# Nine of a trunk's projections read their 512 moving columns, and write their bank, in another order

## The chip, the cores and the metric

One core of a Trainium2 chip runs the whole program. The time is device microseconds of one execution; the median of three runs of the kernel before is 717.47 us (717.14 to 718.04). One further execution was recorded by the hardware profiler. Engines are named as in its profile: PE is TensorE's matmuls, PEld its loads of the stationary operand, DVE is VectorE, ACT is ScalarE, POOL is GpSimd, SP is SyncE.

## The reference

A trunk of two layers on a sequence of 512 tokens of width 1024: a Mamba-2 mixer, then a differential attention layer on shared keys and values, and a last norm. Cut to what the change touches, the mixer's input projection and what becomes of its parts:

```python
h = rms_norm(x, norm_g)
zxbcdt = h @ w_in                         # (512, 1024) @ (1024, 6176)
z   = zxbcdt[..., :2048]                  # the gate
xbc = zxbcdt[..., 2048:2048 + 4096]       # x, B and C of 8 groups
dt_raw = zxbcdt[..., 2048 + 4096:]
xbc = silu(causal_depthwise_conv(xbc, conv_w, conv_b))
...
y = ssd_chunked_scan(xs * dt[..., None], a * dt, bm, cm)
y = gated_group_rms_norm(y + d_skip * xs, z, gate_norm_g)
x = x + y @ w_out
```

All in float32. The attention layer that follows computes `softmax(A1) - lambda * softmax(A2)` on its scores, and is not touched.

## The kernel before

Every large product is made of three matmuls of rounded operands. Weights and activations are split into a high part (`whi`, `a_hi`), which is the value rounded to the type `float32r`, and the rest (`wlo`, `a_lo`). `mm3` (line 242) adds high by high, high by low and low by high into one bank of PSUM. A matmul has a stationary operand of 128 x 128 (`lhsT`), which a weight load brings in, and a moving one of 128 partitions and up to 512 columns (`rhs`); its 128 x 512 result fills one bank.

The gate projection is done in four parts, z0 to z3, each of 512 features (`z_proj`, line 475). For each of four blocks of 128 tokens a bank `pz` is filled: stationary are 128 tokens of the activations, moving are the 512 columns of a weight tile, over eight slices of the depth, so 4 x 8 x 3 = 96 matmuls in a part. ACT reads such a bank in two halves of 256 columns (`z_out`).

The group projection is done for eight groups, g0 to g7 (`group_proj`, line 498). For each of four blocks of 128 features (B, C and two halves of x) a bank `pg` is filled, the other way round: stationary are 128 columns of a weight tile, moving are the 512 tokens of the activations, again 96 matmuls in a group. `conv` then has DVE multiply the bank by a row of scales in place, and ACT and DVE make the causal convolution from it, which needs the tokens in order.

Both write into banks of the tag `mm`, of which there are four. The order of the dense work is the list `order_a`: z0 g0 g1 z1 g2 g3 z2 g4 o0 g5 z3 g6 g7 o1 o2 o3, where o0 to o3 are parts of the out projection (`po`). Around it the scan of each group (`ssd`) puts its small matmuls in between, by a scheduler which works from priorities and estimated times. z0 is partly written out by hand ahead of this list. The weights come by DMA from SP's queue, two or three pieces ahead; ACT makes their high part and DVE the rest.

The names of the profile's rows are the tiles': `pg<-a_hi,whi` is a matmul into a bank of a group projection from the high activations (moving) and the high weights (stationary), while in `pz<-whi,a_hi` the weights move. The operands are given moving first. All TensorE instructions have the one line 55, that of a helper which passes them on, so the rows are told apart by tiles.

Of the kernel before, what the change touches and what calls it, by code (L numbers as in the profile page):

```python
# [37 lines left out]

C_GA, C_GK, C_GB, C_GG, C_SG, C_DTB, C_AL, C_CB, C_CW = 0, 8, 16, 24, 40, 41, 42, 43, 75
N_PAR = 203  # L40

N_DEC = R * NQ * P + 2 * R

# [20 lines left out]
def trunk(ctx, tc, x, x_t, par, w_dt, w_in, w_out, w_kvqg, w_bo, d_skip, lam_qk, fin_g, out):  # L64
# [10 lines left out]
    def mm_bank(name):  # L75
        return psum.tile([P, 512], F32, tag="mm", name=name, bufs=4)
# [22 lines left out]
    nc.scalar.dma_start(prm[:], par[:, 0:C_CB])  # L99
    prc = const.tile([P, N_PAR - C_CB], F32, name="prc")  # L100
    x_tok = res.tile([P, NT, D], F32, name="x_tok")
# [23 lines left out]
    def load(i):  # L125
# [33 lines left out]
        if i == 0:  # L159
# [12 lines left out]
            for i in range(2, 4):  # L172
                nc.sync.dma_start(xt[i], x_t[:, 2 * i:2 * i + 2, :])
                nc.sync.dma_start(nxt[:, 2 * i - 4:2 * i - 2, :].rearrange("p k n -> p (k n)"), src1[:, (2 * i - 4) * w:(2 * i - 2) * w])
            nc.sync.dma_start(prc[:], par[:, C_CB:N_PAR])
        elif i not in begun:
# [15 lines left out]
    def use(seg):  # L192
        fetch(segs.index(seg) + 3)
        return ready.pop(seg)
# [44 lines left out]
                at = 0  # L239
            yield n  # L240

    def mm3(ps, lhs, rhs, first, last, **kw):
        (lh, ll), (rh, rl) = lhs, rhs
        T.matmul(ps, lhsT=lh, rhs=rh, start=first, stop=False, **kw)
        T.matmul(ps, lhsT=lh, rhs=rl, start=False, stop=False, **kw)
        T.matmul(ps, lhsT=ll, rhs=rh, start=False, stop=last, **kw)
# [94 lines left out]
    def new_h(tag):  # L341
        return [res.tile([P, KD, S], F32R, tag=f"hT_{i}", name=f"{tag}_{i}") for i in ("hi", "lo")]


    def tok_mm(ps, t, b, w):
        tk = slice(t * P, (t + 1) * P)
        for k in range(4):
            kk = 4 * b + k
            mm3(ps, (hh[:, kk, tk], hl[:, kk, tk]), (w[0][:, k, :], w[1][:, k, :]), b == 0 and k == 0, b == 1 and k == 3)
            yield  # L350

    hh, hl = new_h("a")
# [10 lines left out]
    def z_out(j, t, ps):  # L363

        for i in range(2):
            zs = bp2.tile([P, 256], F32, tag="zs", name=f"zs{j}_{t}_{i}", bufs=12)
            A.activation(zs, ps[:, i * 256:(i + 1) * 256], AF.Silu, scale=r_col[:, t:t + 1])
            zt[2 * j + i, t] = zs
# [15 lines left out]
    first = load(0)()  # L384
# [8 lines left out]
    for k in range(4):  # L393
        for t in range(NT):
            tk = slice(t * P, (t + 1) * P)
            mm3(pz0[t], (hh[:, k, tk], hl[:, k, tk]), (wh[:, k, :], wl[:, k, :]), k == 0, False)
# [64 lines left out]
    for t in range(NT):  # L461
        run(tok_mm(pz0[t], t, 1, w0))
        z_out(0, t, pz0[t])
# [11 lines left out]
    def z_proj(j):  # L475
        pz = [mm_bank(f"pz{j}_{t}") for t in range(NT)]
        for b in range(2):
            w = use(("z", j, b))
            for t in range(NT):
                yield from tok_mm(pz[t], t, b, w)  # L480
                if b:
                    z_out(j, t, pz[t])

    def conv(ps, ft, name, bufs):
        xc = bp2.tile([P, S], F32, tag=f"xc_{name}", name=f"xc{ft}", bufs=bufs)
        at = C_CW - C_CB + 4 * ft
        cw = [prc[:, at + k:at + k + 1] for k in range(4)]

        u = ps
        V.tensor_tensor(out=u, in0=ps, in1=r_row, op=ALU.mult)  # L490
        A.activation(xc, u, AF.Identity, scale=cw[3], bias=prc[:, ft:ft + 1])
        for k in (2, 1, 0):
            d = 3 - k
            V.scalar_tensor_tensor(out=xc[:, d:], in0=u[:, :S - d], scalar=cw[k], in1=xc[:, d:], op0=ALU.mult, op1=ALU.add)
        A.activation(xc, xc, AF.Silu)
        return xc

    def group_proj(g):
        pg = [mm_bank(f"pg{g}_{i}") for i in range(4)]
        fts = [(16 + g, "b", 1), (24 + g, "c", 2), (2 * g, "x0", 1), (2 * g + 1, "x1", 1)]  # L500
        outs = []
        for b in range(2):
            wh, wl = use(("g", g, b))
            for i in range(4):
                cs = slice(i * P, (i + 1) * P)
                for k in range(4):
                    kk = 4 * b + k
                    mm3(pg[i], (wh[:, k, cs], wl[:, k, cs]), (hh[:, kk, :], hl[:, kk, :]),
                        b == 0 and k == 0, b == 1 and k == 3)
                    yield  # L510
                if b:
                    outs.append(conv(pg[i], *fts[i]))
        conv_out[g] = outs
# [20 lines left out]
    def stream_a():  # L534
        for it in order_a[1:]:
            j = int(it[1])
            yield from {"z": z_proj, "g": group_proj, "o": out_proj}[it[0]](j)
            done.add(it)
        while True:
            yield  # L540
# [136 lines left out]
    hh, hl = new_h("b")  # L677
# [323 lines left out]
    last = None  # L1001
    for h in range(DH):
        for t in range(NT):
# [14 lines left out]
            last = h, t  # L1018
# [135 lines left out]
```

## Time and profile before

| what | value |
|---|---|
| time, median of 3 runs | 717.47 us (717.14 to 718.04) |
| time of the profiled execution | 716.54 us |
| its span, first to last instruction | 714.8 us |
| instructions in the span | 10905 |
| DMA, mean over the span | 99 GB/s |

How to read the rows that are shown below. A line of the page's first part has an engine's busy time, its share of the span and the number of instructions. The lines of the chain follow the work that ended last back to the start, and give each engine's and each tile's share of the span. A row of the waits has who waited for whom, the sum in us, how often, and the longest. A row of a group has line, engine, operation, tiles, shapes and count, then the busy time in us, the mean duration of one in ns, and the idle time before. A row of the timeline has start and duration in us, then the instruction. Matmuls overlap in a pipeline, and the profile models their ends, so two successive starts say more of TensorE's pace than a duration does. A row of the windows has a stretch of the span and each engine's busy time in it.

### The profile page before, as it was taken

The numbers are of one execution on the slowest core, as the hardware profiler recorded it, in microseconds if no ns is written. First come the engines' busy times: TensorE is split into PE (matmuls) and PEld (weight loads), VectorE is DVE, ScalarE is ACT, GpSimd is POOL, SyncE is SP. The second block draws the span as 40 slices with busy tenths as digits, with TensorE's granted clock in tenths as the row PEclk, the third lists the DMA queues.
The fourth block names the chain that finished last, engine by engine and source line by source line (L and its number), as shares of the span: only waits on it lengthen the run. The fifth ranks groups of instructions, "written<-read, shape, count | busy, mean of one in ns | idle before, by whom it ended". The sixth has DMA issues, their size and how long they took to land.

```text
span 714.8 us, 10905 instructions
## 1 busy us (share of the span) xinstructions
PE 705.8 (99%) x4030; PEld 590.2 (83%) x4030; DVE 520.0 (73%) x1195; ACT 429.9 (60%) x953; POOL 113.6 (16%) x158
## 2 busy tenths in 40 slices
PE   8999999999999999999999999999999999999996
PEld 7788888888888888888888879888988898889884
DVE  5579954889579569567996857567667857785886
ACT  6849662754734536537536357667767766756556
POOL 0108512403306025041110101000000000000002
PEclk9999999999999999999999999999999999999999
DMA  8643323233223331331222310412311131122003
GB/s 297 250 175 121 119 73 132 90 119 118 63 114 118 119 117 61 118 119 59 64 85 89 118 59 18 161 66 67 110 61 60 63 116 59 60 89 89 30 0 118
DMA packets 13061, 70.88 MB, mean 99 GB/s; under 512 B 1744, under 2 KB 2512, under 8 KB 5584
## 3 DMA queue, kind: packets, MB, share of 16 engines
q1 hardware_dynamic: 12720, 69.90, 27.3%
q8 instruction: 32, 0.52, 0.3%
q10 hardware_dynamic: 288, 0.28, 0.1%
q14 instruction: 21, 0.17, 0.1%
HBM read 68.02 MB, written 2.16 MB: 98 GB/s over the span
## 4 chain that ended last, share of the span: by engine, by line
PE 96%; DVE 1%; DMA 1%; ACT 0%; issue 0%; SPq 0%
PE pg L55 25%; PE po L55 16%; PE pz L55 12%; PE pt L55 8%; PE pv L55 6%; PE pq L55 6%; PE pk L55 6%; PE pb L55 3%; PE sc L55 3%; PE pyd L55 2%; PE pc L55 2%; PE pcb L55 1%; PE pxt L55 1%; PE psA L55 1%; PE pyt L55 1%; DMA xt<-in_x_t 1%
## 5 line engine op out<-in xcount | busy, mean ns | idle before, releaser
L55 DVE SCALAR_TENSOR_TENSOR wlo<-raw,prm,whi 128x512 fp32r<-128x512 f32 (+1 forms) x256 | 150.5, 636 | 56.3 <-ACT whi L55 56.0
L55 ACT ACTIVATE whi<-raw,prm 128x512 fp32r<-128x512 f32 (+1 forms) x256 | 136.8, 606 | 64.7 <-issue 13.8
L55 PE MATMUL pg<-a_hi,whi 128*128 128x512 f32 x256 | 103.4, 404 | 0.0
L55 PE MATMUL pg<-a_lo,whi 128*128 128x512 f32 x256 | 102.5, 400 | 0.0
L55 PE MATMUL pg<-a_hi,wlo 128*128 128x512 f32 x256 | 101.3, 401 | 0.0
L55 DVE SCALAR_TENSOR_TENSOR xc<-pg,prc,xc 128x511 f32<-128x511 f32 (+2 forms) x96 | 69.9, 740 | 7.5 <-ACT xc L55 7.1
L55 PEld LDWEIGHTS pg<-a_hi,wlo 128*128 128x128 f32 x256 | 48.1, 188 | 11.1
L55 PEld LDWEIGHTS pg<-a_hi,whi 128*128 128x128 f32 x256 | 48.2, 188 | 11.1 <-ACT zs L55 0.2
L55 PEld LDWEIGHTS pg<-a_lo,whi 128*128 128x128 f32 x256 | 48.2, 188 | 10.9
L55 PE MATMUL po<-whi,yh 128*128 128x512 f32 x128 | 51.2, 400 | 0.4 <-ACT yh L55 0.4
L55 PE MATMUL po<-wlo,yh 128*128 128x512 f32 x128 | 51.3, 401 | 0.0
L55 PE MATMUL po<-whi,yl 128*128 128x512 f32 x128 | 50.6, 399 | 0.0
L55 PE MATMUL pz<-wlo,a_hi 128*128 128x512 f32 x128 | 50.1, 400 | 0.0
L55 PE MATMUL pz<-whi,a_hi 128*128 128x512 f32 x128 | 49.4, 400 | 0.5 <-ACT a_hi L55 0.5
L55 PE MATMUL pz<-whi,a_lo 128*128 128x512 f32 x128 | 49.4, 395 | 0.0
L965 POOL TENSOR_TENSOR ot<-x_tok,fg 128x512 f32<-128x512 f32 x4 | 5.0, 1298 | 248.0 <-DVE x_tok L55 248.0
L55 ACT ACTIVATE s<-s,mx 128x128 f32<-128x128 f32 (+3 forms) x64 | 35.5, 556 | 9.6 <-DVE mx L55 9.1
L592 POOL TENSOR_TENSOR xe<-xdt,tok 128x256 f32<-128x256 f32 x24 | 14.1, 613 | 164.1 <-DVE xdt L55 164.1
L55 ACT ACTIVATE xc<-pg,prc 128x512 f32<-128x512 f32 x32 | 24.8, 776 | 24.7 <-DVE pg L55 19.5
L55 DVE CUSTOM_DVE_ANT_0 s<-sc,bias 128x128 f32<-128x128 f32 (+3 forms) x64 | 29.3, 487 | 11.9 <-PE sc L55 11.5
L55 PE MATMUL pv<-whi,b_hi 128*128 128x256 f32 x128 | 36.6, 286 | 0.0
L55 PE MATMUL pv<-wlo,b_hi 128*128 128x256 f32 x128 | 35.7, 279 | 0.0
(238 smaller groups left out, 1678.9 us busy)
## 6 DMA issues: line engine op xcount, KB each, us to landing
raw<-in_w_in SPq DMA_DIRECT2D x22, 1024.0 KB, 4.8
raw<-in_w_kvqg SPq DMA_DIRECT2D x16, 1024.0 KB, 4.7
dec<-acs_d SPq DMA_DIRECT2D x8, 1024.0 KB, 4.8
raw<-in_w_out SPq DMA_DIRECT2D x8, 1024.0 KB, 4.7
raw<-in_w_bo SPq DMA_DIRECT2D x4, 1024.0 KB, 4.8
x_tok<-in_x SPq DMA_DIRECT2D x4, 512.0 KB, 8.8
out<-ot SPq DMA_DIRECT2D x7, 256.0 KB, 2.4
raw<-in_w_in SPq DMA_DIRECT2D x4, 256.0 KB, 4.9
```

Source lines behind the costliest of these rows:

```text
L55: i = op(*args, **kw)
L592: GP.tensor_tensor(out=xe[:, c], in0=xdt[:, c], in1=toe_tok[:, c, hs].unsqueeze(2).to_broadcast([P, R, HD]), op=ALU.mult)
L965: GP.tensor_tensor(out=o, in0=y, in1=f, op=ALU.mult)
```

## The change

`mm3` gets an optional form, a pair (b, c). With it, the moving operand (high and low) and the bank are viewed in another order: the 512 columns are cut into a x b runs of c neighbouring columns, a = 512 / (b c), and the walk goes over b outside, over a in the middle, and over the c columns of a run inside. Moving columns and bank columns are permuted alike, so each result lands where it did. With (2, 4), for instance, a matmul takes columns 0 to 3, 8 to 11, 16 to 19 and so on to the end, and then 4 to 7, 12 to 15 and so on. With (16, 16) it takes 0 to 15, 256 to 271, 16 to 31, 272 to 287 and so on.

Three gate projections (z1, z2, z3) and six group projections (g1 to g6) get a form; z0, g0, g7 and all else stay as they are.

| projection | z1 | z2 | z3 | g1 | g2 | g3 | g4 | g5 | g6 |
|---|---|---|---|---|---|---|---|---|---|
| form (b, c) | 2, 4 | 2, 16 | 16, 16 | 2, 8 | 2, 4 | 2, 32 | 32, 8 | 2, 16 | 2, 128 |
| runs in a matmul, 512 / c | 128 | 32 | 32 | 64 | 128 | 16 | 64 | 32 | 4 |

```diff
+FORM_Z = {1: (2, 4), 2: (2, 16), 3: (16, 16)}
+FORM_G = {1: (2, 8), 2: (2, 4), 3: (2, 32), 4: (32, 8), 5: (2, 16), 6: (2, 128)}
...
-    def mm3(ps, lhs, rhs, first, last, **kw):
+    def walk(ap, form):
+
+        b, c = form
+        return ap.rearrange("p (a b c) -> p b a c", b=b, c=c)
+
+    def mm3(ps, lhs, rhs, first, last, form=None, **kw):
         (lh, ll), (rh, rl) = lhs, rhs
+        if form:
+            ps, rh, rl = walk(ps, form), walk(rh, form), walk(rl, form)
         T.matmul(ps, lhsT=lh, rhs=rh, start=first, stop=False, **kw)
...
-    def tok_mm(ps, t, b, w):
+    def tok_mm(ps, t, b, w, form=None):
...
-            mm3(ps, (hh[:, kk, tk], hl[:, kk, tk]), (w[0][:, k, :], w[1][:, k, :]), b == 0 and k == 0, b == 1 and k == 3)
+            mm3(ps, (hh[:, kk, tk], hl[:, kk, tk]), (w[0][:, k, :], w[1][:, k, :]), b == 0 and k == 0, b == 1 and k == 3, form)
...
-                yield from tok_mm(pz[t], t, b, w)
+                yield from tok_mm(pz[t], t, b, w, FORM_Z.get(j))
...
-                        b == 0 and k == 0, b == 1 and k == 3)
+                        b == 0 and k == 0, b == 1 and k == 3, FORM_G.get(g))
```

On TensorE the program before has, where g1 ends and z1 begins (with two matmuls of a scan, `po`, in between), these rows; a row's last part is the shape of what is moved.

```order
L55 MATMUL pg_3_633<-a_hi,wlo_545 128x512
L55 MATMUL pz_0_918<-whi_636,a_hi 128x512
L55 MATMUL po_735<-hst_684,xc_585 128x256 x2
L55 MATMUL pz_0_918<-wlo_637,a_hi 128x512
L55 MATMUL pz_0_918<-whi_636,a_lo 128x512
```

The changed program has at the same place:

```order
L58 MATMUL pg_3_633<-a_hi,wlo_545 128x2x32x8
L58 MATMUL pz_0_918<-whi_636,a_hi 128x2x64x4
L58 MATMUL po_735<-hst_684,xc_585 128x256 x2
L58 MATMUL pz_0_918<-wlo_637,a_hi 128x2x64x4
L58 MATMUL pz_0_918<-whi_636,a_lo 128x2x64x4
```

No row moved. Line numbers shift, and 512 columns have become three loops, 2 x 32 x 8 in g1 and 2 x 64 x 4 in z1. It is the same along all of TensorE: 864 matmuls have another shape, and their order, like that of every other engine's instructions and of the DMAs, is the order of before.

## The prediction

> **What bounds the kernel now.** I read the page's first part, then its chain, then the waits of TensorE, to see whether a nanosecond on a matmul is a nanosecond on the end.
>
> ```profile
> PE 705.8 (99%) x4030; PEld 590.2 (83%) x4030; DVE 520.0 (73%) x1195; ACT 429.9 (60%) x953; POOL 113.6 (16%) x158
> ```
>
> ```profile
> PE 96%; DVE 1%; DMA 1%; ACT 0%; issue 0%; SPq 0%
> PE pg L55 25%; PE po L55 16%; PE pz L55 12%; PE pt L55 8%; PE pv L55 6%; PE pq L55 6%; PE pk L55 6%; PE pb L55 3%; PE sc L55 3%; PE pyd L55 2%; PE pc L55 2%; PE pcb L55 1%; PE pxt L55 1%; PE psA L55 1%; PE pyt L55 1%; DMA xt<-in_x_t 1%
> ```
>
> ```profile
> PE warm L55 <- POOL ident masks.py:199: 1.5, 1, 1.5
> PE pz L55 <- ACT a_hi L55: 0.5, 1, 0.5
> PE po L55 <- ACT yh L55: 0.4, 1, 0.4
> ```
>
> The chain that ended last is TensorE for 96% of the span, and all that TensorE ever waits for is 1.5 + 0.5 + 0.4 = 2.4 us, none of it inside a projection that the change touches (the 0.5 stands before the first gate projection, z0). The chain's share of "issue" is 0%, so fetching or decoding matmuls is not what sets their pace. The two families that change, `pg` (group projections) and `pz` (gate projections), hold 25% and 12% of the chain. So what counts is the time from one matmul's start to the next one's (the pitch) in these families.
>
> The clock cannot be the lever, because it is granted almost in full:
>
> ```profile
> core 0: 714.8 us, clock 0.998
> ```
>
> The durations on the page (about 400 ns for 512 columns) overlap each other, so I take the pitch from the timeline, first and last row of an undisturbed stretch:
>
> ```profile
> 39.76 0.40 PE L55 MATMUL pg<-a_hi,whi 128*128 128x512 f32 x1
> ...
> 43.96 0.40 PE L55 MATMUL pg<-a_hi,whi 128*128 128x512 f32 x1
> ```
>
> There are 18 steps between these rows: 4.20 / 18 = **233.3 ns** for 512 columns, 0.456 ns a column.
>
> **How many matmuls change.**
>
> ```profile
> L55 PE MATMUL pg<-a_hi,whi 128*128 128x512 f32 x256 | 103.4, 404 | 0.0
> L55 PE MATMUL pg<-a_lo,whi 128*128 128x512 f32 x256 | 102.5, 400 | 0.0
> L55 PE MATMUL pg<-a_hi,wlo 128*128 128x512 f32 x256 | 101.3, 401 | 0.0
> ...
> L55 PE MATMUL pz<-wlo,a_hi 128*128 128x512 f32 x128 | 50.1, 400 | 0.0
> L55 PE MATMUL pz<-whi,a_hi 128*128 128x512 f32 x128 | 49.4, 400 | 0.5 <-ACT a_hi L55 0.5
> L55 PE MATMUL pz<-whi,a_lo 128*128 128x512 f32 x128 | 49.4, 395 | 0.0
> ```
>
> `pg` has 3 x 256 = 768 matmuls in 8 projections, `pz` 3 x 128 = 384 in 4: 96 in each. Six of the one and three of the other change: 9 x 96 = **864 matmuls**, 864 x 233.3 = 201.6 us of the kernel. Nothing else does. The number of instructions, their order, the weight loads, the waits, the transfers and the addresses of every result stay. Each of these 864 reads its 512 moving columns and writes its 512 bank columns in another order, by three loops in place of one. DVE and ACT then read the same banks in order of address, as before, so their groups have no term.
>
> **The cost of one walked matmul.** No row of before shows a matmul with a broken walk, on either side. I bound it by the nearest rows.
>
> From above: a matmul in which a column takes longer exists in the trace, in the unrounded products of the scan.
>
> ```profile
> 118.50 0.40 PE L55 MATMUL pg<-a_hi,whi 128*128 128x512 f32 x1
> 118.74 0.59 PE L55 MATMUL psA<-xe,bt 128*128 128x256 f32 x2
> 118.98 0.58 PE L55 MATMUL pg<-a_lo,whi 128*128 128x512 f32 x1
> 119.40 0.59 PE L55 MATMUL psA<-xe,bt 128*128 128x256 f32 x2
> ```
>
> From 118.74 to 119.40 lie two `psA` records and one `pg` matmul: 0.66 - 0.23 = 0.43 us, 0.21 us for 256 columns, 0.83 ns a column. At that rate 512 columns take 427 ns, 194 more than now. If every walked matmul fell to it, it would cost 864 x 194 = 168 us; if only the two forms with runs of 4 did (z1 and g2, 192 matmuls), 37 us.
>
> From below: the same kind of matmul runs faster elsewhere.
>
> ```profile
> 666.30 0.39 PE L55 MATMUL pb<-whi,oh 128*128 128x512 f32 x1
> ...
> 668.79 0.39 PE L55 MATMUL pb<-whi,ol 128*128 128x512 f32 x1
> ```
>
> Eleven steps, 2.49 / 11 = 226.4 ns, 7 ns under `pg`, with the same shapes, a moving operand from the same pair of weight tiles as `pz` and another stationary one. A comparison with half the columns says where the excess sits:
>
> ```profile
> 431.88 0.28 PE L55 MATMUL pv<-wlo,b_hi 128*128 128x256 f32 x1
> ...
> 433.88 0.28 PE L55 MATMUL pv<-whi,b_hi 128*128 128x256 f32 x1
> ```
>
> Seventeen steps, 2.00 / 17 = 117.6 ns for 256 columns. So 233.3 - 117.6 = 115.7 ns for 256 more columns, 0.452 ns a column, and 2 ns are left for the matmul itself. The time is paid by the column. Against half of the `psA` column (0.83 / 2 = 0.417 ns, if such a column takes two steps of the array, an estimate), some 0.035 ns a column, 18 ns a matmul, look like a stream that is not quite fed or not quite taken. That excess is what a walk can make worse or better: 0 to -18 ns a matmul downwards, 0 to -15.6 us in all.
>
> I take **0 ns**, the nearest row being the matmul itself: same engine, same tiles, same number of columns, and every run is at least 4 columns long and starts at a multiple of 4. Nothing hides a cost here: TensorE is the bound, so a nanosecond more on each is 864 x 1 = 0.86 us at the end.
>
> The Trainium skill, in "PSUM — Partial Sum Buffer", section Specifications (TRN2), says that any access pattern that is not contiguous slows matmuls significantly. In "Advanced Engine Details and Errata", section Memory Cachelines, it repeats this and adds that every two consecutive elements should be contiguous for best throughput, which all nine forms keep. By the first wording the sum is that of the slower rival below or more, by the second it is 0; no row of before decides between them.
>
> **The sum.** The profiled execution took 716.54 us (span 714.8, 1.74 around it). 716.54 + 864 x 0 = 716.54. It lies 0.93 (0.13%) under the median of the three runs, 717.47. Since the forecast is no change, I give the median: **717.5 us**. About 0.2% (1.43 us) is what a measurement of this kernel can tell from none; that is 1.43 / 864 = 1.7 ns a matmul, which is narrow beside the 7 ns by which like matmuls differ already.
>
> **What is late next.** If TensorE slows, every producer has more time and no new wait appears. If it gets faster, the weights must keep up:
>
> ```profile
> core 0: us, PE busy (x) PEld busy (x) DVE busy (x) ACT busy (x) POOL busy (x), PEclk, DMA share, GB/s
> 54.10:82.30 28.20, 28.20 (x188) 23.21 (x187) 26.71 (x42) 22.35 (x31) 17.30 (x24) 1.00 0.39 143
> ...
> 82.50:107.60 25.10, 25.10 (x119) 20.62 (x118) 16.57 (x34) 17.43 (x31) 9.23 (x10) 1.00 0.18 59
> 107.80:135.70 27.90, 27.90 (x181) 22.85 (x181) 17.85 (x30) 10.28 (x21) 11.65 (x17) 1.00 0.37 134
> ...
> sum 243.10, PE 243.10 PEld 199.78 DVE 177.94 ACT 137.27 POOL 78.57; mean PE 27.01 PEld 22.20 DVE 19.77 ACT 15.25 POOL 8.73
> ```
>
> These are the stages of g1, z1, g2 and the sum of all nine walked projections. Only in g1 is DVE near full (26.71 of 28.20), so a gain of over 1.5 us there would be eaten; the sum (177.94 of 243.10) leaves room for the rest. With 96 x 18 = 1.7 us as the most that one projection can gain, the passage is nearly one to one both ways.
>
> **The rivals.**
>
> *Slower: a run's first column costs more.* Each jump to another place interrupts the stream, on the read or on the bank side, and the price goes by the number of runs. A matmul has 512 / c runs: 128, 32 and 32 in z1 to z3, 64, 128, 16, 64, 32 and 4 in g1 to g6, 500 in all, times 96 = 48,000 runs. At one more column time each (0.456 ns) that is +21.9 us, 739.4 us from the median. It decides from 1.43 us / 48,000 = 0.03 ns a run. For it: the stream already loses time by the column, so it has no slack to absorb a jump. Against it: no row shows a cost that goes with jumps, and a run of 4 or more could still be fed at the present rate. The first wording of the skill's PSUM page is on its side. A harsher form, in which runs of 4 fall to the `psA` rate, gives 717.47 + 37.2 = 754.7.
>
> *Faster: the excess goes.* If the 18 ns come from neighbouring columns asked for one after the other, or from a standing clash with the weight load beside it, another order may lose it. At the `pb` pitch (226.4) the gain is 864 x 6.9 = 6.0 us, 711.5 us. At the estimated floor it is 15.6 us, 701.9. For it: `pb` shows that the excess depends on something other than shape. Against it: the pitch holds at 233 across very different neighbours, and only some of nine unlike forms should hit a good order.
>
> *The change is not what it says.* If the loops were folded back into one, the time would be 717.5 as well. The built program shows the three loops, so I give this nothing of its own.
>
> **How the numbers follow.** No change: 0.40. Slower: 0.37, of which about 0.25 between +1.4 and +22 us and 0.12 beyond. Faster: 0.23, of which 0.17 down to the `pb` pitch and 0.06 beyond. The range leaves out the two outer parts, 0.18 in all: from 717.5 - 6.5 = 711 to 717.5 + 22.5 = 740. The forecast's own range is 716.0 to 718.9. Chances: faster 0.23, same 0.40, slower 0.37.
>
> **What would show it.** In the timeline of the changed kernel the pitch in each walked projection, with z0, g0 and g7 as controls in the same execution: 233 ns throughout would confirm the term. A pitch that rises with 512 / c (most in z1 and g2, least in g6) is the slower rival, and its slope is the price of a jump; one that falls towards 226 or less is the faster one. If z1 and g2, which have one form but swap the roles of weights and activations, differ, the side that matters is the moving tile. The forecast is wrong if the mean pitch of the 864 moves by more than 1.7 ns, or if TensorE's waits grow beyond 2.4 us.

## The result, and the profile after

The changed kernel takes 720.8 us (median of 8 runs), the kernel before 717.75 (8 runs, the first three among them). The ratio is 1.0051, with a 95% interval from 1.0037 to 1.0065: **slower by 0.5%**, 3.05 us between the medians. Seven of its eight runs lie between 720.29 and 721.25 us; the eighth took 727.32 us at a lower granted clock (0.993, against 0.997 to 0.998). The profiled execution took 720.31 us, its span is 718.5, 3.7 more than before.

TensorE is the bound as before, by the page's first part, the chain by engine, and TensorE's waits:

```profile
PE 709.0 (99%) x4030; PEld 590.5 (82%) x4030; DVE 520.5 (72%) x1195; ACT 430.0 (60%) x953; POOL 113.5 (16%) x158
```

```profile
PE 91%; DVE 2%; DMA 2%; ACT 2%; issue 1%; SPq 1%; POOL 0%; ACTq 0%; POOLq 0%
```

```profile
PE warm L58 <- POOL ident masks.py:199: 1.5, 1, 1.5
PE pxt L58 <- ACT xc L58: 0.6, 1, 0.6
PE po L58 <- ACT yh L58: 0.4, 1, 0.4
PE pz L58 <- ACT a_hi L58: 0.3, 1, 0.3
```

3.2 of the 3.7 us are TensorE's busy time (709.0 against 705.8), and one wait of 0.6 us, for ACT before a transpose `pxt`, is new. The chain has more of other engines than before (TensorE 91% in place of 96%), since it is followed back through that wait into what ACT had waited for (45.4 to 65.2 us), and since its first 28.4 us now run through DMA and POOL, where before they ran through z0 from 8.6 us on. The timeline says where the busy time went. Each fence has first and last row of an undisturbed stretch: g7, the control, which has no form; g2 with (2, 4), the most runs; g1 with (2, 8); g5 with (2, 16); g4 with (32, 8).

```profile
327.43 0.40 PE L58 MATMUL pg<-a_hi,whi 128*128 128x512 f32 x1
...
333.03 0.40 PE L58 MATMUL pg<-a_hi,whi 128*128 128x512 f32 x1
```

```profile
128.53 0.40 PE L58 MATMUL pg<-a_lo,whi 128*128 128x512 f32 x1
...
134.13 0.40 PE L58 MATMUL pg<-a_lo,whi 128*128 128x512 f32 x1
```

```profile
56.86 0.39 PE L58 MATMUL pg<-a_lo,whi 128*128 128x512 f32 x1
...
61.49 0.39 PE L58 MATMUL pg<-a_lo,whi 128*128 128x512 f32 x1
```

```profile
254.36 0.40 PE L58 MATMUL pg<-a_hi,whi 128*128 128x512 f32 x1
...
260.11 0.40 PE L58 MATMUL pg<-a_hi,whi 128*128 128x512 f32 x1
```

```profile
191.02 0.41 PE L58 MATMUL pg<-a_hi,whi 128*128 128x512 f32 x1
...
196.83 0.41 PE L58 MATMUL pg<-a_hi,whi 128*128 128x512 f32 x1
```

Four of the stretches have 24 steps, that of g1 20. g7: 5.60 / 24 = 233.3 ns. g2, with 128 runs in a matmul: 5.60 / 24 = 233.3, no dearer at all. g1, 64 runs: 4.63 / 20 = 231.5, cheaper. g5, 32 runs: 5.75 / 24 = 239.6. g4, 64 runs: 5.81 / 24 = 242.1. Worked out in the same way for all nine:

| projection, form | runs | pitch, ns | against 233.3 |
|---|---|---|---|
| z1 (2, 4) and g2 (2, 4) | 128 | 233.3, 233.3 | 0, 0 |
| g1 (2, 8) | 64 | 231.5 | -1.8 |
| z2 (2, 16), g5 (2, 16) | 32 | 240.0, 239.6 | +6.7, +6.3 |
| g3 (2, 32) | 16 | 235.4 | +2.1 |
| g6 (2, 128) | 4 | 233.3 | 0 |
| z3 (16, 16) | 32 | 240.0 | +6.7 |
| g4 (32, 8) | 64 | 242.1 | +8.8 |

The sum of the last column is 28.8 ns; times 96 matmuls each it is 2.8 us. That is nearly all of the measured 3.05. The windows of the same stages, g1, z1, g2 and the sum of the nine, show the rest:

```profile
core 0: us, PE busy (x) PEld busy (x) DVE busy (x) ACT busy (x) POOL busy (x), PEclk, DMA share, GB/s
54.20:83.10 28.90, 28.34 (x188) 23.17 (x187) 28.00 (x43) 23.08 (x31) 17.77 (x23) 1.00 0.40 146
83.30:108.40 25.10, 25.10 (x120) 20.63 (x118) 16.98 (x34) 17.47 (x33) 9.53 (x10) 1.00 0.19 58
108.60:136.50 27.90, 27.90 (x181) 22.84 (x180) 17.41 (x29) 9.83 (x21) 11.19 (x16) 1.00 0.36 134
...
sum 246.70, PE 246.14 PEld 200.31 DVE 179.38 ACT 138.11 POOL 79.01; mean PE 27.35 PEld 22.26 DVE 19.93 ACT 15.35 POOL 8.78
```

z1 and g2 are as long as they were (25.10 and 27.90). g1 is 0.7 longer although its matmuls are faster: TensorE is idle there for 28.90 - 28.34 = 0.56 us, the new wait. DVE is at 28.00 of 28.90 in that stage.

### The profile page after: what moved, and what is told of

Same layout as the page of the kernel before. It is cut to its first block, busy times and chain, and to the rows that moved or that the text cites. A ratio compares the mean times of both kernels' runs of the same rounds, so it can differ in the third digit from the quotient of the medians.

```text
span 718.5 us, 10901 instructions
## 1 busy us (share of the span) xinstructions
PE 709.0 (99%) x4030; PEld 590.5 (82%) x4030; DVE 520.5 (72%) x1195; ACT 430.0 (60%) x953; POOL 113.5 (16%) x158
## 4 chain that ended last, share of the span: by engine, by line
PE 91%; DVE 2%; DMA 2%; ACT 2%; issue 1%; SPq 1%; POOL 0%; ACTq 0%; POOLq 0%
PE pg L58 23%; PE po L58 16%; PE pz L58 10%; PE pt L58 7%; PE pv L58 6%; PE pq L58 6%; PE pk L58 6%; PE pb L58 3%; PE sc L58 3%; PE pyd L58 2%; PE pc L58 2%; DMA x_tok<-in_x 1%; DMA xt<-in_x_t 1%; PE pxt L58 1%; PE psA L58 1%; PE pyt L58 1%
```

## The experiments

Eleven kernels were run. In all of them z0, g0 and g7 serve as controls; their pitch stayed at 232 to 235 wherever it was not itself changed. Pitches are given as the median over a projection, from start to start, or from two quoted rows.

### Which side pays: the read or the bank?

The first two kernels have the change's nine forms, with `sides` either the read or the bank; the other side keeps its order of address:

```diff
-        b, c = form
-        return ap.rearrange("p (a b c) -> p b a c", b=b, c=c)
+        b, c, sides = form
+        if side in sides:
+            return ap.rearrange("p (a b c) -> p b a c", b=b, c=c)
+        return ap.rearrange("p (b a c) -> p b a c", b=b, c=c)
...
-            ps, rh, rl = walk(ps, form), walk(rh, form), walk(rl, form)
+            ps, rh, rl = walk(ps, form, "bank"), walk(rh, form, "read"), walk(rl, form, "read")
```

> The nine forms of the change, but for the moving operand alone; the banks are written from the first column to the last, so the columns of these nine projections come out permuted. In the changed kernel the median pitch (start to start) was 240 to 242 ns in z2, z3, g4 and g5, 236 in g3, 232 in g1 and 232.5 to 234 in z1, g2 and g6, against 233 to 235 before. Theory READ (the jumps cost where the moving operand is fetched): these medians come back within 1 ns, z2, z3, g4, g5 at 240 to 242. Theory BANK (they cost where the sums are written): all nine stand at 233 to 235 as before. If both sides share the cost, z2, z3, g4, g5 lie in between, at 236 to 239.

> The mirror image: the nine forms for the banks alone, the moving operand read from its first column to its last, results permuted. Theory READ: 233 to 235 ns in all nine. Theory BANK: z2, z3, g4, g5 at 240 to 242, g3 at 236, g1 at 232.

The timeline of g4 with the moving operand alone walked:

```profile
191.09 0.41 PE L58 MATMUL pg<-a_hi,whi 128*128 128x512 f32 x1
...
196.90 0.41 PE L58 MATMUL pg<-a_hi,whi 128*128 128x512 f32 x1
```

and with the bank alone walked:

```profile
191.00 0.40 PE L58 MATMUL pg<-a_hi,whi 128*128 128x512 f32 x1
...
196.60 0.40 PE L58 MATMUL pg<-a_hi,whi 128*128 128x512 f32 x1
```

24 steps each: 5.81 / 24 = 242.1 ns, the pitch of the changed kernel, against 5.60 / 24 = 233.3, the pitch of before. So it is in the other projections: read alone gives 241 in z2, 240 in z3 and g5, 236 in g3, 231.5 in g1; bank alone gives 232 to 235 in all nine. In one run each, beside 718.24 for the kernel before, the first took 720.46 us and the second 718.21. **The cost and the gain sit wholly on the moving operand's side**, and writing a bank in runs of 4 to 128 columns, as in these nine forms, costs nothing.

The bank-only kernel also waited 0.9 us for ACT before `pxt`, with g1's matmuls at their old pitch; in two later kernels whose g1 was untouched (the stepped weight load and the fewer weights) the wait was 1.2 and 0.3. So that wait does not come from g1's form. Eleven of the twelve kernels profiled beside the one before have it, at 0.3 to 1.5 us; the one before was profiled once, without it. Whether it varies from one execution to the next or goes with every changed program is not shown.

### Run length or distance?

The same change with other forms (both sides walked, results in place):

```diff
-FORM_Z = {1: (2, 4), 2: (2, 16), 3: (16, 16)}
-FORM_G = {1: (2, 8), 2: (2, 4), 3: (2, 32), 4: (32, 8), 5: (2, 16), 6: (2, 128)}
+FORM_Z = {1: (4, 4), 2: (8, 4), 3: (64, 4)}
+FORM_G = {1: (4, 4), 2: (8, 4), 3: (16, 4), 4: (32, 4), 5: (64, 4), 6: (2, 2)}
```

> Both sides walked, runs of 4 columns (16 bytes) in seven of the nine forms, so 128 runs a matmul, at growing distance: (4,4) in z1 and g1, (8,4) in z2 and g2, (16,4) in g3, (32,4) in g4, (64,4) in z3 and g5; and runs of 2 in g6, (2,2). Theory DISTANCE (a jump costs 0.14 to 0.21 ns where it lands 64 bytes or more behind the end of the last run, and nothing where it lands nearer, as the changed kernel's forms (2,16), (16,16), (32,8), (2,32) against (2,4), (2,8) suggest): (4,4) skips 48 bytes and stays at 232 to 235 ns; (8,4) to (64,4) have 128 such jumps and stand at 251 to 262. Theory LENGTH (the length of a run alone sets it, 16 columns worst, 4 and 8 free): all runs of 4 at 232 to 235 at any distance. Theory COUNT, the slower rival of the prediction (0.456 ns a run): already fallen for (2,4), it would give 292. For (2,2) DISTANCE gives 232 to 235.

In the timeline, z1 with (4, 4), g3 with (16, 4) and three rows of g6 with (2, 2):

```profile
86.80 0.38 PE L58 MATMUL pz<-wlo,a_hi 128*128 128x512 f32 x1
...
92.08 0.38 PE L58 MATMUL pz<-wlo,a_hi 128*128 128x512 f32 x1
...
136.62 0.44 PE L58 MATMUL pg<-a_hi,whi 128*128 128x512 f32 x1
...
143.32 0.45 PE L58 MATMUL pg<-a_hi,whi 128*128 128x512 f32 x1
...
317.62 0.65 PE L58 MATMUL pg<-a_hi,whi 128*128 128x512 f32 x1
318.07 0.65 PE L58 MATMUL pg<-a_lo,whi 128*128 128x512 f32 x1
318.53 0.65 PE L58 MATMUL pg<-a_hi,wlo 128*128 128x512 f32 x1
```

Over 24 steps each, (4, 4) takes 5.28 / 24 = **220.0 ns** and (16, 4) takes 6.70 / 24 = **279.2**; (2, 2) takes 0.46 us. A distance is counted here from the start of one run to the start of the next. With runs of 4 columns throughout, the median was 221 (z1) and 225.5 (g1) at a distance of 64 bytes, 252 and 243 at 128, 278 at 256, 265 at 512 and 247 to 253 at 1024. LENGTH falls, since one length gives 220 to 279. DISTANCE, as I had put it, falls too: the price does not begin at 64 bytes and stay; (4, 4) is the fastest form of all, and I had expected 232 to 235. Runs of two columns, 8 bytes, take about twice the time; since both sides were walked, this run does not tell whether the read or the bank makes them do so.

```diff
+FORM_Z = {1: (2, 8), 2: (4, 8), 3: (32, 8)}
+FORM_G = {1: (2, 4), 2: (4, 8), 3: (8, 8), 4: (16, 8), 5: (4, 16), 6: (8, 16)}
```

> Both sides walked, runs of 8 and 16 at other distances: (2,8) in z1, (4,8) in z2 and g2, (8,8) in g3, (16,8) in g4, (32,8) in z3, (4,16) in g5, (8,16) in g6, (2,4) in g1. Theory DISTANCE: (2,8) skips 32 bytes and stands at 232 as in g1 of the changed kernel; (4,8), (8,8), (16,8), (32,8) have 64 jumps over 96 bytes or more and stand at 242 to 247; (4,16) and (8,16) have 32 and stand at 238 to 241. Theory LENGTH: runs of 8 at 232 at any distance (but (32,8) stood at 242 in the changed kernel), runs of 16 at 240. In g1 with (2,4) the wait of 0.6 us for ACT, which the changed kernel had in g1 with (2,8), is there again if it comes from the changed times of earlier work, and is gone if the form (2,8) made it.

Medians: (2, 8) 233, (4, 8) 230 and 229, (8, 8) 244, (16, 8) 230, (32, 8) 244, (4, 16) 240, (8, 16) 233. Both theories fail again: (4, 8) and (16, 8) are 3 to 4 ns under the contiguous walk, (8, 8) and (32, 8) 11 ns above. No rule for runs longer than four columns comes out of these runs. The wait for ACT before `pxt` was there (0.7 us) with (2, 4) in g1.

### The best form everywhere

```diff
+        form = (4, 4)
+        ps, rh, rl = walk(ps, form), walk(rh, form), walk(rl, form)
         T.matmul(ps, lhsT=lh, rhs=rh, start=first, stop=False, **kw)
```

> The best form found, (4,4), on both sides of all split matmuls of the program: pg, pz, po, pk, pq, pt, pb, pc with 512 columns and pv with 256. With (4,4) the pitch was 221 ns in z1 (weights move) and 225.5 in g1 (activations move), against 234 before. If the gain holds in every family: pz 384 x 13 + pg and pk, pq, pt 1344 x 9 + po 384 x 13 + pb, pc 192 x 5 + pv 384 x 5 ns = 5.0 + 12.1 + 5.0 + 1.0 + 1.9 = 25 us, so 693 us if every other engine keeps up. If DVE and ACT (73% and 60% of the span before, DVE 26.7 of 28.2 us in g1) become the bound in places, part of it is lost to waits of TensorE: 695 to 705. If the gain hangs on the addresses of z1 and g1 alone, other families stay at 227 to 234 and the whole at 705 to 712.

The median of four runs is 702.89 us beside 717.91 for the kernel before (9 runs); ratio 0.9793, interval 0.978 to 0.9807: **2.1% faster than the kernel before**, a gain of 15.0 us where I had written 25. The gain I had written was carried over from the best medians of two projections. By the mean pitch of each family, start to start under 330 ns in both traces, it is 10.5 ns in pz, 6.1 in pg, 6.5 in pk, 5.4 in pq, 6.3 in pt, 3.3 in po, 3.4 to 3.5 in pb and pc and 2.0 in pv; times 384, 768, three times 192, 384, twice 96 and 384 matmuls that is 14.9 us. TensorE's waits grew from 2.4 to 4.7 us in all. 14.9 less these 2.3 is 12.6 us, and the profiled execution, the slowest of the four (704.04 us), is 12.5 us under that of before. So most of what is missing is on TensorE, whose matmuls gain less by the mean than by the medians of z1 and g1, and the smaller part is lost to waits.

```diff
+    const.tile([P, 8], F32, name="pad")
     prm = const.tile([P, C_CB], F32, name="prm")
```

> The same as the kernel with (4,4) everywhere, with a pad of 32 bytes at the start of on-chip memory, so that every later tile lies 32 bytes further and the distance between any two of them stays. Before the shift the moving weights start at a multiple of 64 bytes and the moving activations 32 bytes behind one; after it this is the other way round. Theory START (a matmul's pitch depends on where its own moving operand starts): pg goes from 225 to 221 and pz from 221 to 225. Theory DISTANCE BETWEEN THE TWO (it depends on how moving and stationary operand lie to each other): pz and pg stay at 221 and 225. In all: START with more columns on the side of the activations (1344 against 960 matmuls) gives 1 to 2 us less than the kernel without the pad.

703.41 us, median of five runs, ratio 0.98 (0.9786 to 0.9813): the same, since its runs (702.98 to 703.83) lie within those without the pad (702.39 to 704.04). z1 to z3 stayed at 220 to 221 and g1 to g4 at 225. START falls. What makes the weights, as moving operand, 5 ns faster than the activations is not their own start address; whether it is the distance to the stationary operand, the theory that is left, no run shows.

### The weight load beside it

The stationary operand is not walked in three loops here, but stepped:

```diff
+    def stepped(t, st):
+        return slice(t // st * P * st + t % st, (t // st + 1) * P * st, st)
...
-        tk = slice(t * P, (t + 1) * P)
+        tk = stepped(t, st)
```

> The stationary operand is taken in steps: every second or every fourth column of a wider stretch, so that a weight load of 128 columns touches 2 or 4 times as many 16-byte pieces; rows of the results are permuted among the four banks of a projection. z1 and g2: step 2, moving operand as before. z2 and g3: step 4, as before. z3 and g4: step 4 with moving (4,4). g5: step 2 with moving (2,16). g6: moving (4,4) alone. g1: untouched. Theory CLASH (the excess over 215 ns comes from weight load and moving operand meeting in the same part of memory): z1, g2 and more so z2, g3 leave the 233 to 235 of before by over 3 ns, upwards if more pieces mean more meetings; z3 and g4 leave 221 and 225. Theory SELF (the moving operand's own order sets it): z1, z2, g2, g3 at 233 to 235, z3 at 221, g4 and g6 at 225, g5 at 240. In g1, which is as in the kernel before, TensorE's wait of 0.6 us for ACT is there again if it is a matter of the single execution.

The timeline of z3 (step 4, moving operand (4, 4)):

```profile
296.34 0.40 PE L58 MATMUL pz<-whi,a_lo 128*128 128x512 f32 x1
...
300.60 0.39 PE L58 MATMUL pz<-whi,a_lo 128*128 128x512 f32 x1
```

18 steps, 4.26 / 18 = 236.7 ns where (4, 4) alone had 220; in g4 the median is 237, where it was 225. With the moving operand read in order, the medians are 236 in z2 and g3 (step 4) and 233 and 232 in z1 and g2 (step 2). So step 2 costs nothing, and with step 4 all four projections have a median of 236 to 239, whether the moving operand is walked or not. The expectation of over 3 ns for the contiguous walk was not met: it rose by 2 or so. In g5, (2, 16) with step 2, the median is 241, against 240.

A clash between load and matmul is not needed to explain the step of 4, because the loads themselves became long. These are the rows of a weight load in the kernel before, in the stretch of z3 above, and, from the next kernel, of a load of 32 columns:

```profile
L55 PEld LDWEIGHTS pg<-a_hi,whi 128*128 128x128 f32 x256 | 48.2, 188 | 11.1 <-ACT zs L55 0.2
L58 PEld LDWEIGHTS pz<-whi,a_lo 128*128 128x128 f32 x6 | 1.9, 319 | 0.0
L58 PEld LDWEIGHTS pg<-a_lo,whi 128*32 128x32 f32 x128 | 14.0, 109 | 14.8 <-issue 4.3
```

With step 4 a load takes 319 ns and the loads follow each other without any idle time. From 32 to 128 columns a load grows from 109 to 188 ns, 0.82 ns a column, so some 83 of the 188 ns do not go with the columns (an estimate, on a straight line). 319 - 83 = 236 ns is the pitch of the stretch; for z2, g3 and g4 the same estimate gives 227 to 238 beside 236 and 237. With step 2 a load takes 195 to 197 ns, and the pitch stays. So the likeliest reading is that the loads with step 4 set the pace themselves; that they slow the matmul beside them is not shown.

```diff
+        T.matmul(ps if first else ps[0:n], lhsT=lh if first else lh[:, 0:n], rhs=rh, start=first, stop=False, **kw)
+        T.matmul(ps[0:n], lhsT=lh[:, 0:n], rhs=rl, start=False, stop=False, **kw)
+        T.matmul(ps if last else ps[0:n], lhsT=ll if last else ll[:, 0:n], rhs=rh, start=False, stop=last, **kw)
```

> All but the first and last matmul of each bank load 64 or 32 stationary columns in place of 128, which leaves out part of the sums in the other rows of the bank; the moving operand has its 512 columns. z1 and g5: 64 columns; z2 and g2: 32; z3 and g6: 32 with moving (2,16); g3: 32 with moving (16,4); g4: 32 with moving (4,4); g1: untouched. Theory CLASH: the excess over 215 ns shrinks with the weight load: from 234 to about 225 with 64 columns and 220 with 32; (2,16) from 240 to about 222 and (16,4) from 278 to about 231. Theory SELF: 233 to 235 with 64 and with 32, 240 with (2,16), 278 with (16,4), 225 with (4,4).

g3, (16, 4) with 32 stationary columns (the rows' 128*32):

```profile
140.66 0.44 PE L58 MATMUL pg<-a_lo,whi 128*32 128x512 f32 x1
...
147.28 0.44 PE L58 MATMUL pg<-a_hi,whi 128*32 128x512 f32 x1
```

24 steps, 6.62 / 24 = 275.8 ns, against 279.2 with the full load. (2, 16) stays at 237 and 238 (240, 241 before), (4, 4) in g4 goes from 225 to 221. The contiguous walk has 231 and 233 with 64 columns, 230 in z2 and 238 in g2 with 32. CLASH had asked for 220 to 231; the price of a walk hardly depends on the weight load, so **the moving operand's own order sets nearly all of it**. Between contiguous walks and short loads this run gives no clear answer, since one of four rose.

### A map of distances

Here each moving operand is read in runs of 4 columns at one constant distance, from the whole tile:

```diff
+    def strided(flat, form):
+
+        s, m = form
+        n = 128 // m
+        return flat[:, 0:n * s].rearrange("p (a m c) -> p m a c", a=n, c=4)[:, 0:m]
```

> Moving operands are read in 128 runs of 4 columns (16 bytes) at one constant distance, without any return, from the whole tile of activations or weights; banks are written from first to last. The products of these nine projections are of other columns than the reference's. Distances in bytes from run to run: z1 32, g1 and z2 48, g2 and z3 64, g3 80, g4 96, g5 112, g6 128. Theory PERIOD (places a multiple of 256 bytes apart share a part of memory, and runs that follow each other there wait, 0.5 ns each: (16,4) has 7 of 8 steps at 256 bytes and stood at 278 ns, (32,4) 3 of 4 at 512 and 265, (64,4) 1 of 2 at 1024 and 247 to 253): 48 to 112 bytes all stand at 219 to 227 ns, as (4,4) with 64 did; 128 bytes returns to the same part at every second run and stands at 243 to 255; 32 bytes at 233 to 234 as (2,4). Theory LONG (a jump costs the more, the longer it is): the pitch rises steadily from 64 bytes to 128, with 80, 96 and 112 between 225 and 250.

> The same with four passes of 32 runs of 4 columns at a greater constant distance, products again of other columns: g1 and z2 240 bytes, g2 and z3 256, g3 272, g4 384, g5 496, g6 512. z1 is untouched. Theory PERIOD: 256 and 512 bytes stand at 275 to 285 ns; 384 (a multiple of 128) at 243 to 255; 240, 272 and 496, which lie only 16 bytes off a multiple of 256, at 219 to 236. Theory LONG: all of them at 250 to 285, whatever the remainder.

> The two distances that stood out, 80 bytes (267 ns) and 96 bytes (320 ns), once in four passes of 32 runs, as far from run to run but over a stretch four times shorter (z1 and g1: 96 bytes, z2 and g2: 80), and once as before in one pass, but with 32 stationary columns loaded in place of 128 in all but the first and last matmul of a bank (g3: 80 bytes, g4: 96), which leaves out part of the sums. z3 and g5: 64 bytes in four passes, g6: 128 bytes in four passes. Products are of other columns than the reference's. Theory MAP (the distance from run to run sets the price): z1, g1 at 310 to 320 ns, z2, g2 at 260 to 267, g6 at 245 to 260, z3 and g5 at 221 to 226 as with (4,4), which has the same order. Theory REACH (a pass over 8 to 16 KB costs, not the distance): z1, g1, z2, g2 fall to 225 to 245. Theory CLASH with the weight load: g3 and g4 fall by more than half of their excess, to under 240 and under 268; if the moving operand's order alone sets it they stay within 5 ns of 267 and 320.

Rows of g4 with 96 bytes (near distances, one pass):

```profile
192.69 0.48 PE L58 MATMUL pg<-a_hi,whi 128*128 128x512 f32 x1
...
200.36 0.49 PE L58 MATMUL pg<-a_hi,whi 128*128 128x512 f32 x1
```

and of g2 with 256 bytes and g3 with 272 (far distances, four passes):

```profile
132.16 0.45 PE L58 MATMUL pg<-a_lo,whi 128*128 128x512 f32 x1
...
138.97 0.45 PE L58 MATMUL pg<-a_lo,whi 128*128 128x512 f32 x1
...
142.09 0.40 PE L58 MATMUL pg<-a_hi,whi 128*128 128x512 f32 x1
...
147.61 0.39 PE L58 MATMUL pg<-a_hi,whi 128*128 128x512 f32 x1
```

24 steps each: 7.67 / 24 = 319.6 ns, 6.81 / 24 = 283.8 and 5.52 / 24 = 230.0. Sixteen bytes further, and 54 ns a matmul are gone. The medians, with one pass or four:

| distance, bytes | 32 | 48 | 64 | 80 | 96 | 112 | 128 |
|---|---|---|---|---|---|---|---|
| one pass | 233 | 226, 228 | 235, 239 | 267 | 320 | 233 | 260 |
| four passes | | | 221, 225 | 271, 272 | 313, 313 | | 249 |

| distance, bytes | 240 | 256 | 272 | 384 | 496 | 512 |
|---|---|---|---|---|---|---|
| four passes | 236, 240 | 284, 287 | 233 | 249.5 | 236 | 284 |

PERIOD is right for the far distances: multiples of 256 cost 284 to 287, 384 stands where 128 does in four passes, and the three that lie 16 bytes off are near the contiguous pitch (233 to 240). LONG falls. But PERIOD gave 219 to 227 for all distances from 48 to 112 bytes, and in one pass only 48 stands about there; 96 is the dearest of the whole list, and 80 comes next after 96 and the multiples of 256. The prices of 80 and 96 are not an effect of the long stretch (four passes over a quarter of it cost nearly the same, 271 to 272 and 313, so REACH falls for them), nor of the weight load (32 columns: 267 and 320, unchanged), nor of the kind of operand (313 in z1 and in g1). At 64 and 128 bytes, however, one long pass costs 10 to 18 ns more than four short ones. So MAP stands as a description, to within some 18 ns: the distance from one run of 16 bytes to the next sets the pitch, and 80 and 96 came out alike in two kernels. What gives them their price is open. 64 bytes in four passes is the read of (4, 4), here with the banks written in order, and it has the same 221 and 225 ns: the gain of (4, 4), too, is the read's.

## Why the prediction was off

- **TensorE as the bound, with nearly all passed on to the end: right.** 2.8 us by the nine pitches beside 3.05 measured; the controls did not move.
- **The term 864 x 0 failed.** The step was to take the matmul itself as nearest row, on the ground that every run is at least 4 columns long and starts at a multiple of 4. For three of the nine projections that holds (z1, g2, g6); one is 1.8 ns cheaper, five cost 2.1 to 8.8. The mean is 28.8 / 9 = 3.2 ns, against the 1.7 that I had named as the edge of what can be seen. By that sign of my own the forecast was wrong: the term was mis-sized, and 720.8 lies 1.9 us above the forecast's own range of 716.0 to 718.9. The wide range of 711 to 740 held it, but it reached there by the price of the slower rival, whose mechanism fell, so this is luck in part. The two kernels with one side walked show what stands in the term's place: a cost of the order in which the moving operand is read. Why each of the nine orders has its price stays open.
- **The slower rival had the right sign by the wrong mechanism.** Its price by the number of runs would have been highest in z1 and g2. These have 128 runs and cost nothing, while 32 runs cost 6.7 ns. Of the two sides it named, only the read counts. Its harsher form rested on a misread row: the kernel issues 16 `psA` matmuls and the trace has 32 records, two for each, so the 0.43 us are one matmul of 256 columns, 1.7 ns a column in place of 0.83. No matmul of the change came near either.
- **The faster rival was closer to the mechanism than the forecast.** It said that the 18 ns over an even feed come from the order in which neighbouring columns are asked for, and that another order may lose them. (4, 4), which the change does not contain, loses 13 of them in the projections where the weights move. I had held it back because nine unlike forms would rarely hit a good order; in fact only (2, 8) gained, a little.
- **The estimated floor was not passed.** 233.3 less the 18 ns is 215 ns for 512 columns; the best pitch of the runs is 220.0. That a column of a `psA` record takes two steps, on which the 18 ns rest, no run shows.
- **"If z1 and g2 differ, the moving tile matters"** did not show it: they do not differ with (2, 4). With (4, 4) they do, 221 against 225.
- **The wait for ACT before `pxt`** in g1 was not foreseen. It is 0.6 us in the profiled execution and was 0.3 to 1.2 in three kernels without a walked read in g1, so g1's walked read does not make it. With it TensorE's waits came to 2.8 us, beyond the 2.4 that I had named as a sign of being wrong.

The Trainium skill, in "PSUM — Partial Sum Buffer", section Specifications (TRN2), has any pattern that is not contiguous slow a matmul. For the banks of this kernel the measurement speaks against it: 232 to 235 ns with nine broken walks over the banks alone. In "SBUF — State Buffer", section Specifications (TRN2), it gives on-chip memory lines of 16 bytes, asks for at least two hits in a line for full bandwidth, and has each crossing to a new line pay a penalty. Runs of 8 bytes have two hits in a line and took 453 ns, about twice 233.3; as the banks were walked in the same runs, that run does not tell whether two hits are too few. (4, 4) goes to a new line as often as the contiguous walk, and took less, 220.0 ns, so by this trace the number of crossings alone does not set the price.

## What to carry to other kernels

Where matmuls on rounded float32 follow each other without a gap, measure the pitch from start to start per 512 columns: if it is near the 233 ns of this kernel, the order in which the moving operand is read is worth a try (it came to 221 to 227 in the gate and group projections), and permuting moving columns and bank columns alike keeps the result in place. Here runs of 16 bytes at 64 bytes' distance, all through the program, took 2.1% off the time of a kernel that seemed full; distances of 80, 96 or a multiple of 256 bytes make a matmul up to 37% longer. A cost that seems to go by the number of pieces should be tried at several distances first, on one side at a time.

## What the runs showed of the hardware that was not expected

The contiguous walk is not the fastest read: 233.3 ns for 512 columns, against 220.0 with (4, 4). A weight load of every fourth column takes 310 to 325 ns in place of 188, and the projections with it stand at 236 to 239 ns whatever the moving order, while one of every second column takes 195 to 197 ns and costs nothing at the end. And the pitch of a read at 96 bytes' distance, 313 to 320 ns, is nearly the same for weights and activations, in one pass or four, with 128 or 32 stationary columns.
